# The convolution's bias as a row of its bands, its windows in parts of 32 and 30 rows, and LayerNorm's affine part on VectorE

## The chip, the cores and the metric

The kernel is one program on one core of a Trainium2 chip. The metric is the device time of one execution in microseconds (us), as the median of several runs; smaller is better.

## What is computed

The reference is one inference step of a two-layer backbone: 256 context tokens and 1024 latent tokens, model width 1024. The change lies in the first (even) layer, in its convolution branch and in what stands around it:

```python
a_u, a_g, a_z, b_q, b_k, b_v, b_z = jnp.split(h @ w_in, SPLIT_E, axis=-1)   # A_W = 512 each, b_*: 512 each
a = a_u * jax.nn.sigmoid(a_g)
a = lax.conv_general_dilated(a, conv_w[:, None, :], window_strides=(1,),     # CONV_K = 31, one filter a channel
                             padding=[(15, 15)], dimension_numbers=('NWC', 'WIO', 'NWC'),
                             feature_group_count=A_W) + conv_b
a = jax.nn.silu(layer_norm(a, ln_g, ln_b)) * jax.nn.silu(a_z)
...
o = over_query_blocks(lambda qb: diff_attend(qb, keys, vals, lam), q)        # from b_q, b_k, b_v
return jnp.concatenate([a, o * jax.nn.silu(b_z)], axis=-1) @ w_out

def layer_norm(x, g, b):
    mu, var = mean(x), mean(square(x - mu))
    return (x - mu) * rsqrt(var + 1e-6) * g + b
```

The second layer and all attention code are the same in both kernels.

## The kernel before

The tokens are ten tiles of 128 (tiles 0 and 1 context, 2 to 9 latent). The input stage of the first layer is `l0_in`. It multiplies the normed tokens with seven groups of weight columns: two groups `ug0` and `ug1` (a_u and a_g of 256 channels each), `az` (weights `w6`), and four heads (weights `w2` to `w5`). Each group is eight 128x512 weight chunks; each chunk is loaded by SP (`raw_w`, L263), rounded by ScalarE (L269), and its low part is cut by GpSimd (`w_w`, L270). TensorE works unit by unit: a unit is one token tile (or one channel block) and has 24 matmuls into one of five `acc` buffers of PSUM, three for each chunk (L318 to L320, or L330 to L332). The names in a profile row are `acc_v` (a head's value and gate columns of a token tile), `acc_p` (a context tile), `acc_c` (channel blocks of q and k). A unit's result is taken out of PSUM by ScalarE (`cn` L492, `vz` L509) and VectorE (`gz` L340, `ch` L494 and L495), which frees the buffer. `hl` (L357) is VectorE's part of the split of a context tile's q and k, which TensorE transposes (`tr_st`, L360).

Between the units a generator is stepped (`filler`, `branch`): first `conv`, at 4/3 step a unit, then `ln_steps`, at `LNR` steps a unit. `modulation` vectors for later stages (`md_v`, `modv`, L162, from `rawm_v` loads) are stepped beside it.

`conv` works in eight blocks `q` of 64 channels. The gated values, split in a high and a low part, are stored to DRAM (`AW0`, `AW1`; `ahl` L416 and L417, store L420, two `ahl` buffers) with padding rows. `windows(q)` loads windows of 64 rows, 32 rows apart, 21 times 2 of them, back into SBUF (`X`, two buffers): high parts in partitions 0 to 63, low parts in 64 to 127, in four DMAs. A band matrix (`band`, built on the host from the filter) has 64 rows of which 62 are not zero, and 32 columns; one matmul for each channel (L471) gives 32 outputs of each window. ScalarE and VectorE add the two halves (`cy`, L476 and L477), and ScalarE's queue stores the block to DRAM (`CV`). The values stay doubled there, since the gate is computed as (tanh + 1) times u.

`ln_steps` then loads CV by token tile (`lnw`, L571), and for each tile: halves it and adds the bias `convb` (L575), statistics (L577, L579, L580) and the root on GpSimd (`mv`, L95), `norm` (VectorE L586, ScalarE L587, GpSimd L588), tanh on ScalarE (L609), two gate multiplications on VectorE (L592, L593; the second reads `AZ`, loaded at L585), store to `CAT` (L594).

The program is written out once and a scheduler orders the instructions of each engine with its own simulated times; a queue keeps its order. SP's DMAs use eight completion semaphores in turn, so a DMA also waits for the one eight places ahead.

Of the kernel before, what the change touches and what calls it, by code (L numbers as in the profile page):

```python
# [10 lines left out]
F32 = mybir.dt.float32  # L11
F32R = mybir.dt.float32r
# [20 lines left out]
def f32(ap):  # L33
    return ap.bitcast(F32)
# [42 lines left out]
class K:  # L77
# [323 lines left out]
    def l0_in(self, ws, raw, wp, cxp, p1, small, acc, pst, mod, freed):  # L401
# [8 lines left out]
        def ug_units(gi):  # L410
# [10 lines left out]

            return [(f"ug{gi}_{t}", self.mm_tok(t), lambda ps, t=t: done(t, ps)) for t in TORD]

        def conv():

            raws, bands = [], []  # L430

            def windows(q):
                x = cxp.tile([128, CWIN, CCH], F32R, tag="X", bufs=2, name=f"X{q}")
                cs = slice(q % 4 * CCH, q % 4 * CCH + CCH)
                for o in range(2):
                    for hl in range(2):
                        src = self.AW[q // 4][hl, 32 * o : 32 * o + 32 * CWIN, cs].rearrange("(j r) c -> r j c", r=64)
                        dst = x[hl * 64 : hl * 64 + 64].rearrange("p (j o) c -> p o j c", o=2)[:, o]
                        nc.sync.dma_start(f32(dst), f32(src))
                return x  # L440

            def load_taps():
                if len(raws) < 32:
                    raws.append(self.wload(a["toep"][len(raws)], raw, f"band{len(raws)}", "rawb"))

            def cut_taps():
                i = len(bands)
                if i < 32:
                    bands.append(self.wcut(raws[i], cxp, f"band{i}", "band", nc.vector))
                    load_taps()  # L450

            load_taps()
            load_taps()
            yield
            xs = [windows(0)]
            cut_taps()
            yield
            yield
            for q in range(8):
                y = cxp.tile([CWIN, 32, CCH], F32, tag="cy", bufs=1, name=f"cy{q}")  # L460
                x = xs.pop(0)
                for c0 in range(0, CCH, 8):
                    if c0 == 8 and q < 7:
                        xs.append(windows(q + 1))
                    ps = pst(f"cv{q}_{c0}")
                    for i in range(8):
                        c = c0 + i
                        if c % 16 == 0:
                            cut_taps()
                        w = bands[4 * q + c // 16]  # L470
                        nc.tensor.matmul(  # L471
                            ps[0:CWIN, i * 64 : i * 64 + 64].rearrange("p (a m) -> p a m", a=2), x[:, :, c],
                            w[:, :, c % 16 * 32 : c % 16 * 32 + 32], start=True, stop=True)
                    pv = ps[0:CWIN].rearrange("p (c a m) -> p c a m", a=2, m=32)
                    yv = y[:, :, c0 : c0 + 8].rearrange("p m c -> p c m")
                    nc.scalar.copy(yv, pv[:, :, 1])  # L476
                    nc.vector.tensor_tensor(yv, pv[:, :, 0], yv, ALU.add)  # L477
                    if c0 + 8 == CCH:
                        dst = self.CV[:, q * CCH : q * CCH + CCH].rearrange("(w m) c -> w m c", m=32)
                        nc.scalar.dma_start(dst, y)  # L480
                    yield
# [75 lines left out]
        def ln_steps():  # L557

            con = cxp.tile([128, 3, 512], F32, tag="cy", bufs=1, name="lncon")
            for i, nm in enumerate(("lng", "lnb", "convb")):
                nc.sync.dma_start(con[:, i], a[nm].broadcast_to([128, 512]))
            ws = [cxp.tile([128, CWIN * CCH], F32, tag="X", bufs=2, name=f"lnw{i}") for i in range(2)]
            slots = [w[:, i * 512 : i * 512 + 512] for w in ws for i in range(5)]
# [6 lines left out]

            def stats(t):
                u = us[t % 6]
                nc.vector.scalar_tensor_tensor(u, u, 0.5, con[:, 2], ALU.mult, ALU.add)  # L575
                st = small.tile([128, 6], F32, tag="bn", name=f"bn{t}")
                nc.vector.bn_stats(st, u)  # L577
                mvs[t] = mv = small.tile([128, 4], F32, tag="mv", bufs=3, name=f"mv{t}")
                nc.vector.bn_aggr(mv[:, 0:2], st)  # L579
                nc.vector.tensor_scalar(mv[:, 1:2], mv[:, 1:2], EPS, None, ALU.add)  # L580
                self.rsq(mv[:, 2:3], mv[:, 1:2])

            def norm(t):
                u, mv = us[t % 6], mvs[t]
                nc.sync.dma_start(azs[t % 2], self.AZ[t])  # L585
                nc.vector.scalar_tensor_tensor(u, u, mv[:, 0:1], con[:, 0], ALU.subtract, ALU.mult)  # L586
                nc.scalar.activation(u, u, AF.Identity, scale=mv[:, 2:3])  # L587
                nc.gpsimd.tensor_tensor(u, u, con[:, 1], ALU.add)  # L588

            def gate(t):  # L590
                u = us[t % 6]
# [4 lines left out]
            load(0)  # L596
            yield
            load(1)
            yield
            yield  # L600
            for s in range(NT + 3):
                if s >= 3:
# [8 lines left out]
                    stats(s)  # L611
                yield

        convd, credit, RATE, LNR = [], [0.0], 4 / 3, 0.8

        def branch():
            yield from conv()
# [864 lines left out]
def _layout(i):  # L1482
# [38 lines left out]
    band = np.zeros((512, 64, 32), np.float32)  # L1521
    for m in range(32):
        band[:, m : m + 31, m] = i["a_conv_w"][0].T
    band = band.reshape(32, 16, 64, 32).transpose(0, 2, 1, 3).reshape(32, 64, 512)
    z["toep"] = c(np.concatenate([band, band], 1))
    z["convb"] = c(i["a_conv_b"])
    z["lng"], z["lnb"] = c(i["a_ln_g"]), c(i["a_ln_b"])
    z["lamv"] = c(i["b_lambda"][0])
    z["subg"] = c(i["b_subln_g"])
# [52 lines left out]
```

## Time and profile before

| | before |
|---|---|
| time, median of 3 runs | 1827.05 us (1825.0 to 1831.14) |
| time of the profiled execution | 1820.6 us |
| span in its profile | 1818.8 us |
| mean granted TensorE clock | 0.987 |
| busy: TensorE, VectorE, ScalarE, GpSimd | 95%, 68%, 53%, 43% |
| first matmul of the convolution | 137.86 us |
| LayerNorm's first and last instruction on VectorE | 427.22 and 486.37 us |

The times in a profile count from the span's start. A row of the timeline gives start, duration, engine, line, operation, output and input, and in brackets how long the engine had idled before and what released it; in a row of several instructions (x2, x6) the duration covers all. A row of a window gives the busy time of each engine in that stretch, the granted clock (1.00 is full speed), the DMA engines' busy share and GB/s. A group of instructions gives the count, the busy sum in us, the mean of one in ns, and the idle time before them.

### The profile page before, as it was taken

Reading aid. Unit: us, or ns where it says so; the run is one execution under the profiler, and the core shown is the slowest. Engines: PE = TensorE matmul, PEld = TensorE weight load, DVE = VectorE, ACT = ScalarE, POOL = GpSimd, SP = SyncE. Lnnn points to the kernel's source line nnn. Section 1 sums busy time; section 2 is a strip of 40 time slices with the busy share of each in tenths; the row PEclk is TensorE's granted clock in tenths of the full one; section 3 lists DMA queues with packets and bytes.
Section 4 is the critical chain, followed back from the end, with each engine's and each line's share of the span. In section 5 each row is a group of like instructions: output and inputs, shape, how many; then the busy total and the mean of one; then the engine's idle time right before and its main releaser. Section 6 shows DMA issues by size and latency. Waiting matters only on the chain. (4 is left out here: it accounts for less than half of the span.)

```text
span 1818.8 us, 28268 instructions
## 1 busy us (share of the span) xinstructions
PE 1727.2 (95%) x9434; PEld 1420.3 (78%) x9434; DVE 1235.8 (68%) x2935; ACT 972.9 (53%) x2060; POOL 787.8 (43%) x706
## 2 busy tenths in 40 slices
PE   5999999998899999989999999999999999999998
PEld 2787888887777778778887778877888888878786
DVE  7656765676749989925476672118899989999322
ACT  6433344342437778743344533227777888898311
POOL 3321032233627778754138873203344334354332
PEclk9999999999899999999999999999999999999999
DMA  8468888854774433144246345253122114141441
GB/s 304 156 159 198 240 199 186 190 171 140 220 202 112 124 102 96 45 161 152 85 157 183 138 133 157 76 147 100 33 54 58 33 41 108 59 146 58 153 174 52
DMA packets 220277, 241.23 MB, mean 133 GB/s; under 512 B 72128, under 2 KB 154848, under 8 KB 219876
## 3 DMA queue, kind: packets, MB, share of 16 engines
q1 hardware_dynamic: 207476, 233.53, 44.1%
q0 software_dynamic: 1792, 3.15, 0.8%
q10 hardware_dynamic: 10864, 2.75, 0.8%
q8 instruction: 75, 1.23, 0.3%
q14 instruction: 70, 0.57, 0.1%
HBM read 169.08 MB, written 70.28 MB: 132 GB/s over the span
## 5 line engine op out<-in xcount | busy, mean ns | idle before, releaser
L397 ACT ACTIVATE E<-E,mm 128x1536 f32<-128x1536 f32 (+3 forms) x240 | 293.6, 1227 | 59.8 <-DVE E L394 49.9
L270 POOL TENSOR_TENSOR w_w<-raw_w,w_w 128x512 fp32r<-128x512 f32 x88 | 127.1, 1453 | 237.4 <-ACT w_w L269 180.1
L1238 PE MATMUL S<-k1d,q1s 128*128 128x512 f32 (+1 forms) x704 | 206.9, 390 | 4.0 <-DMA q1s<-qT 1.7
L372 POOL TENSOR_TENSOR el<-ef,eh 128x512 fp32r<-128x512 f32 x96 | 124.2, 1295 | 187.7 <-DVE eh L371 182.7
L394 DVE TENSOR_SCALAR_CACHE_REDUCE E<-S,mm 128x512 f32<-128x512 f32 x256 | 190.2, 744 | 12.9 <-PE S L798 3.9
L1168 PE MATMUL wt_et<-ident,E 128*128 128x128 f32 x1264 | 186.1, 273 | 3.7 <-ACT E L397 3.2
L1168 PEld LDWEIGHTS wt_et<-ident,E 128*128 128x128 f32 x1264 | 153.8, 140 | 37.2 <-ACT E L397 4.5
L368 DVE TENSOR_TENSOR el<-wt_et,eh 128x512 fp32r<-128x512 f32 x220 | 146.9, 682 | 10.2 <-ACT eh L367 9.6
L1238 PEld LDWEIGHTS S<-k1d,q1s 128*128 128x128 f32 x704 | 121.4, 190 | 28.5 <-DVE E L394 7.7
L367 ACT CAST eh<-wt_et 128x512 fp32r<-128x512 f32 x220 | 124.3, 595 | 29.1 <-PE wt_et L1168 28.6
L1163 PE MATMUL pv_pv<-el,v 128*128 128x512 f32 x316 | 138.9, 440 | 0.5 <-POOL el L372 0.4
L798 PE MATMUL S<-kd,qs 128*128 128x512 f32 (+1 forms) x416 | 131.6, 422 | 7.8 <-DVE E L394 3.7
L318 PE MATMUL acc_g<-w_w,hi 128*128 128x512 f32 x336 | 131.4, 393 | 1.4 <-DVE v L1021 1.3
L319 PE MATMUL acc_g<-w_w,hi 128*128 128x512 f32 x336 | 132.2, 394 | 0.5 <-POOL w_w L270 0.5
L320 PE MATMUL acc_g<-w_w,lo 128*128 128x512 f32 x336 | 131.7, 392 | 0.0
L1162 PE MATMUL pv_pv<-eh,v 128*128 128x512 f32 x316 | 127.8, 405 | 0.5 <-DVE eh L371 0.5
L873 PE MATMUL acc_po<-wo,oh 128*128 128x512 f32 x320 | 126.2, 395 | 0.0
L874 PE MATMUL acc_po<-wo,oh 128*128 128x512 f32 x320 | 125.5, 393 | 0.0
L394 DVE TENSOR_SCALAR_CACHE_REDUCE E<-S 128x512 f32<-128x512 f32 (+1 forms) x160 | 99.8, 630 | 18.9 <-PE S L1238 12.3
L269 ACT CAST w_w<-raw_w 128x512 fp32r<-128x512 f32 x96 | 59.0, 620 | 90.7 <-DMA raw_w<-in_we 22.7
L877 PE MATMUL acc_po<-wo,ol 128*128 128x512 f32 x320 | 103.1, 393 | 0.0
L798 PEld LDWEIGHTS S<-kd,qs 128*128 128x128 f32 x416 | 67.6, 191 | 30.8 <-DVE E L394 20.9
(294 smaller groups left out, 4550.4 us busy)
## 6 DMA issues: line engine op xcount, KB each, us to landing
rawm_v<-in_wmodt SPq DMA_DIRECT2D x64, 256.0 KB, 2.9
raw_w<-in_we SPq DMA_DIRECT2D x56, 256.0 KB, 3.5
X<-AW SPq DMA_DIRECT2D x32, 336.0 KB, 6.4
qs<-QK SPq DMA_DIRECT2D x80, 128.0 KB, 2.8
ac<-CAT SPq DMA_DIRECT2D x20, 512.0 KB, 4.0
raw_w<-in_wod SPq DMA_DIRECT2D x40, 256.0 KB, 2.7
q1s<-qT SPq DMA_DIRECT2D x40, 256.0 KB, 2.6
xraw_m<-in_wmod SPq DMA_DIRECT2D x32, 256.0 KB, 4.6
```

Source lines behind the costliest of these rows:

```text
L270: (eng or nc.gpsimd).tensor_tensor(w[:, 1, :], r, f32(w[:, 0, :]), ALU.subtract)
L318: nc.tensor.matmul(ps[:, o:], a, w[:, 0, o:], start=(k == 0), stop=False)
L319: nc.tensor.matmul(ps[:, o:], a, w[:, 1, o:], start=False, stop=False)
L320: nc.tensor.matmul(ps[:, o:], b, w[:, 0, o:], start=False, stop=(k == KC - 1))
L368: nc.vector.tensor_tensor(lo, ps, f32(hi), ALU.subtract)
L394: nc.vector.tensor_scalar(e[:, o : o + w], S, -1.0, init, ALU.mult, ALU.min, accum_out=m[:, i : i + 1])
L397: nc.scalar.activation(e[:, :n], e[:, :n], AF.Exp, bias=init, scale=-1.0, accum_out=s)
L798: nc.tensor.matmul(S, q[:, hl], kd[:, c, kofs + o : kofs + o + n], start=(hl == 0), stop=(hl == 1))
L1162: nc.tensor.matmul(pv, vs, wh, start=(i == 0), stop=False)
L1163: nc.tensor.matmul(pv, vs, wl, start=False, stop=(i == nk - 1))
L1168: nc.tensor.transpose(ps[:, g * 128 : g * 128 + 128], E[g][:, ec : ec + 128], self.ident)
L1238: nc.tensor.matmul(S, qs[:, g, :], kd[hl][:, kc : kc + n], start=(hl == 0), stop=(hl == 1))
```

## The change

The bias moves into the band matrix: row 62 of each channel's band, in the high half and the low half alike, holds the channel's bias, and the windows hold 2.0 in row 62 of the high half and 0.0 in row 62 of the low half. The convolution's output is then twice (convolution + bias) without another instruction. The window buffers are allocated once and their rows 32 to 63 and 96 to 127 filled by GpSimd; the window loads leave rows 62 and 63 untouched, and each of the four loads is cut into rows 0 to 31 and 32 to 61. LayerNorm works on the doubled values with four times the epsilon, so that halving and adding the bias go away (and with them the load of `convb`); scale and bias of `norm` become one VectorE instruction in the place of one on ScalarE and one on GpSimd. `LNR` goes from 0.8 to 0.6, and one empty step is left out.

```diff
+        win = [cxp.tile([128, CWIN, CCH], F32R, tag="X", bufs=2, name=f"win{i}") for i in range(2)]
+        for w in win:
+            nc.gpsimd.memset(f32(w[32:64]), 2.0)
+            nc.gpsimd.memset(f32(w[96:128]), 0.0)
...
             def windows(q):
-                x = cxp.tile([128, CWIN, CCH], F32R, tag="X", bufs=2, name=f"X{q}")
+                x = win[q % 2]
...
-                        nc.sync.dma_start(f32(dst), f32(src))
+                        for r in (slice(0, 32), slice(32, 62)):
+                            nc.sync.dma_start(f32(dst[r]), f32(src[r]))
...
-            con = cxp.tile([128, 3, 512], F32, tag="cy", bufs=1, name="lncon")
-            for i, nm in enumerate(("lng", "lnb", "convb")):
+            con = cxp.tile([128, 2, 512], F32, tag="cy", bufs=1, name="lncon")
+            for i, nm in enumerate(("lng", "lnb")):
...
             def stats(t):
                 u = us[t % 6]
-                nc.vector.scalar_tensor_tensor(u, u, 0.5, con[:, 2], ALU.mult, ALU.add)
...
-                nc.vector.tensor_scalar(mv[:, 1:2], mv[:, 1:2], EPS, None, ALU.add)
+                nc.vector.tensor_scalar(mv[:, 1:2], mv[:, 1:2], 4 * EPS, None, ALU.add)
...
                 nc.vector.scalar_tensor_tensor(u, u, mv[:, 0:1], con[:, 0], ALU.subtract, ALU.mult)
-                nc.scalar.activation(u, u, AF.Identity, scale=mv[:, 2:3])
-                nc.gpsimd.tensor_tensor(u, u, con[:, 1], ALU.add)
+                nc.vector.scalar_tensor_tensor(u, u, mv[:, 2:3], con[:, 1], ALU.mult, ALU.add)
...
             load(1)
             yield
-            yield
             yield
...
-        convd, credit, RATE, LNR = [], [0.0], 4 / 3, 0.8
+        convd, credit, RATE, LNR = [], [0.0], 4 / 3, 0.6
...
     band = np.zeros((512, 64, 32), np.float32)
     for m in range(32):
         band[:, m : m + 31, m] = i["a_conv_w"][0].T
+    band[:, 62] = i["a_conv_b"][0][:, None]
...
-    z["convb"] = c(i["a_conv_b"])
```

The scheduler gives another order in `l0_in` alone. On GpSimd the four fills (128 partitions in two parts of 32, 2688 values each) come between the cuts of weight chunks 4 and 5 of group `ug1`; on TensorE the matmuls of chunks 5 to 7 for the token tiles 2 to 4 of that group stand some 40 matmuls further back, and the first convolution block 6 matmuls further ahead (row 440, before 446).

Three more places. First SP's queue at the first window loads. Before (`X0`, `X1` are the windows, `ahl1_2` and `ahl1_3` stores that free the buffers of `ahl1_4` and `ahl1_5`):

```order
L420 DMA AW0_73<-ahl0_0_1092 128x2x256
L263 DMA raw_w6_2_1494<-in_we 128x512
L420 DMA AW0_73<-ahl0_1_1099 128x2x256
L261 DMA rawm_v0_2_4_0_1362<-in_wmodt 128x512
L261 DMA rawm_v0_2_5_0_1416<-in_wmodt 128x512
L439 DMA X0_1135<-AW0_73 64x21x64 x4
L439 DMA X1_1281<-AW0_73 64x21x64 x2
L420 DMA AW1_74<-ahl1_2_1131 128x2x256
L439 DMA X1_1281<-AW0_73 64x21x64
L420 DMA AW1_74<-ahl1_3_1184 128x2x256
L439 DMA X1_1281<-AW0_73 64x21x64
L261 DMA rawm_v0_2_6_0_1481<-in_wmodt 128x512
```

Now, from the last two of 16 window loads on:

```order
L446 DMA win1_740<-AW0_73 32x21x64
L446 DMA win1_740<-AW0_73 30x21x64
L261 DMA rawm_v0_2_5_0_1428<-in_wmodt 128x512
L261 DMA rawm_v0_2_6_0_1493<-in_wmodt 128x512
L263 DMA raw_w6_0_1502<-in_we 128x512
L263 DMA raw_w6_1_1504<-in_we 128x512
L263 DMA raw_w6_2_1506<-in_we 128x512
L420 DMA AW1_74<-ahl1_2_1137 128x2x256
L420 DMA AW1_74<-ahl1_3_1193 128x2x256
```

Two `rawm_v` loads, the three first loads of group `w6` and the two `AW1` stores now stand behind all the window loads.

Second, VectorE from LayerNorm's first instruction on. The row to look for is `gz2_6` (L340), which frees the buffer of `acc_v2_6`. Before, the last 12 rows up to it (27 LayerNorm and `ch` rows stand ahead of it in all):

```order
L577 BN_STATS bn3_4582<-lnw0_4291 128x6
L575 SCALAR_TENSOR_TENSOR lnw1_4292<-lnw1_4292,lncon_4287 128x512
L592 SCALAR_TENSOR_TENSOR lnw0_4291<-lnw1_4292,lnw0_4291 128x512
L579 BN_AGGR mv2_4534<-bn2_4532 128x2
L494 TENSOR_TENSOR ch2_2_1_4431<-cn2_2_1_4473,ropeT_526 128x512
L495 TENSOR_TENSOR ch2_2_0_4430<-cn2_2_1_4473,ropeT_526 128x512
L579 BN_AGGR mv3_4584<-bn3_4582 128x2
L593 SCALAR_TENSOR_TENSOR lnw0_4291<-lnw0_4291,lnw1_4292 128x512
L580 TENSOR_SCALAR mv2_4534<-mv2_4534 128x1
L586 SCALAR_TENSOR_TENSOR lnw0_4291<-lnw0_4291,mv2_4534,lncon_4287 128x512
L577 BN_STATS bn4_4645<-lnw0_4291 128x6
L340 SCALAR_TENSOR_TENSOR gz2_6_4519<-th_z2_6_4520,acc_v2_6_4491 128x128
```

Now (L592 is the first half of `norm`, the new L593 the second; L597 and L598 are the gate):

```order
L583 BN_STATS bn4_4699<-lnw0_4320 128x6
L583 BN_STATS bn5_4829<-lnw1_4321 128x6
L597 SCALAR_TENSOR_TENSOR lnw0_4320<-lnw1_4321,lnw0_4320 128x512
L598 SCALAR_TENSOR_TENSOR lnw0_4320<-lnw0_4320,lnw1_4321 128x512
L501 TENSOR_TENSOR ch2_2_1_4459<-cn2_2_1_4499,ropeT_526 128x512
L502 TENSOR_TENSOR ch2_2_0_4458<-cn2_2_1_4499,ropeT_526 128x512
L593 SCALAR_TENSOR_TENSOR lnw0_4320<-lnw0_4320,mv2_4558,lncon_4317 128x512
L593 SCALAR_TENSOR_TENSOR lnw0_4320<-lnw0_4320,mv3_4606,lncon_4317 128x512
L585 BN_AGGR mv4_4701<-bn4_4699 128x2
L340 SCALAR_TENSOR_TENSOR gz2_6_4545<-th_z2_6_4546,acc_v2_6_4517 128x128
```

`gz2_6` has 30 rows ahead of it instead of 27: 6 statistics (L583), 5 aggregates (L585), 4 one-column additions (L586), 4 first and 4 second halves of `norm`, 3 gate rows and 4 `ch` rows. The `hl` row of the second context tile of head 3 comes 57 rows after `gz2_6`, before 58.

Third, GpSimd where the chunks `w_w5` of the last head are cut among LayerNorm's roots (`mv`). Before:

```order
L95 TENSOR_TENSOR mv4_4647<-mv4_4647,mhalf_65 128x1
L270 TENSOR_TENSOR w_w5_0_4598<-raw_w5_0_4592,w_w5_0_4598 128x512
L270 TENSOR_TENSOR w_w5_1_4615<-raw_w5_1_4594,w_w5_1_4615 128x512
L95 TENSOR_TENSOR mv5_4697<-mv5_4697,mhalf_65 128x1
L270 TENSOR_TENSOR w_w5_2_4632<-raw_w5_2_4596,w_w5_2_4632 128x512
L588 TENSOR_TENSOR lnw0_4291<-lnw0_4291,lncon_4287 128x512
L588 TENSOR_TENSOR lnw1_4292<-lnw1_4292,lncon_4287 128x512
L270 TENSOR_TENSOR w_w5_3_4665<-raw_w5_3_4613,w_w5_3_4665 128x512
L95 TENSOR_TENSOR mv6_4745<-mv6_4745,mhalf_65 128x1
L270 TENSOR_TENSOR w_w5_4_4682<-raw_w5_4_4630,w_w5_4_4682 128x512
L270 TENSOR_TENSOR w_w5_5_4715<-raw_w5_5_4663,w_w5_5_4715 128x512
```

Now:

```order
L95 TENSOR_TENSOR mv4_4701<-mv4_4701,mhalf_65 128x1
L95 TENSOR_TENSOR mv5_4831<-mv5_4831,mhalf_65 128x1
L270 TENSOR_TENSOR w_w5_0_4620<-raw_w5_0_4614,w_w5_0_4620 128x512
L270 TENSOR_TENSOR w_w5_1_4637<-raw_w5_1_4616,w_w5_1_4637 128x512
L270 TENSOR_TENSOR w_w5_2_4654<-raw_w5_2_4618,w_w5_2_4654 128x512
L95 TENSOR_TENSOR mv6_4896<-mv6_4896,mhalf_65 128x1
L270 TENSOR_TENSOR w_w5_3_4671<-raw_w5_3_4635,w_w5_3_4671 128x512
L270 TENSOR_TENSOR w_w5_4_4688<-raw_w5_4_4652,w_w5_4_4688 128x512
L270 TENSOR_TENSOR w_w5_5_4719<-raw_w5_5_4669,w_w5_5_4719 128x512
```

The additions L588 are gone from between the cuts, and the first cut comes one root later.

## The prediction

> **What bounds the kernel now.** I read the page's busy shares first, then TensorE's waits in the stretch of LayerNorm, then that stretch by windows, then the queues row by row.
>
> ```profile
> span 1818.8 us, 28268 instructions
> PE 1727.2 (95%) x9434; PEld 1420.3 (78%) x9434; DVE 1235.8 (68%) x2935; ACT 972.9 (53%) x2060; POOL 787.8 (43%) x706
> ```
>
> TensorE sets the time, so an edit on another engine counts only where TensorE waits for it. The change adds no matmul and takes none away; only TensorE's waits and its clock can move the time. The waits from 430 to 490 us (engine, line, releaser: us, times, longest):
>
> ```profile
> PE acc_v L318 <- DVE gz L340: 6.2, 1, 6.2
> PE acc_c L332 <- POOL w_w L270: 3.7, 2, 2.4
> PE tr_st L360 <- DVE hl L357: 2.5, 1, 2.5
> PE acc_v L318 <- ACT cn L492: 0.7, 1, 0.7
> ```
>
> That is 13.1 us. The clock falls after them, and VectorE is full meanwhile:
>
> ```profile
> 460.00:480.00 20.00, 15.65 (x63) 11.69 (x61) 19.59 (x31) 10.52 (x34) 15.78 (x13) 0.83 0.73 254
> ...
> 444.00:448.00 4.00, 3.65 (x15) 3.45 (x16) 4.00 (x9) 2.02 (x3) 2.89 (x3) 0.50 0.83 260
> ...
> 464.00:468.00 4.00, 2.35 (x6) 1.05 (x5) 3.96 (x7) 2.41 (x12) 4.00 (x4) 0.68 0.92 344
> 468.00:472.00 4.00, 3.94 (x9) 3.15 (x10) 4.00 (x10) 2.23 (x8) 2.64 (x3) 0.50 0.70 228
> ```
>
> (Busy us of TensorE, weight loads, VectorE, ScalarE, GpSimd, then the clock.) At clock 0.50, 3.65 us of matmuls lose 1.8; with 2.35 times 0.32 = 0.75 and 3.94 times 0.5 = 2.0 that makes 4.5 us. So 13.1 + 4.5 = 17.6 us is what LayerNorm's stretch can give back in all.
>
> **The change, part by part.**
>
> *LayerNorm on VectorE.* Rows of VectorE's timeline:
>
> ```profile
> 427.22 0.69 DVE L575 SCALAR_TENSOR_TENSOR lnw<-lnw,lncon 128x512 f32<-128x512 f32 x1 [9.80 <-DMA lnw<-CV]
> 427.94 0.69 DVE L577 BATCH_NORM_STATS2 bn<-lnw 128x6 f32<-128x512 f32 x1
> 428.55 0.67 DVE L575 SCALAR_TENSOR_TENSOR lnw<-lnw,lncon 128x512 f32<-128x512 f32 x1
> 429.15 0.17 DVE L579 BATCH_NORM_AGGREGATE mv<-bn 128x2 f32<-128x6 f32 x1
> 429.26 0.69 DVE L577 BATCH_NORM_STATS2 bn<-lnw 128x6 f32<-128x512 f32 x1
> 429.87 0.14 DVE L580 TENSOR_SCALAR mv<-mv 128x1 f32<-128x1 f32 x1
> 429.93 0.74 DVE L586 SCALAR_TENSOR_TENSOR lnw<-lnw,mv,lncon 128x512 f32<-128x512 f32 x1
> ...
> 432.48 1.69 DVE L575 SCALAR_TENSOR_TENSOR lnw<-lnw,lncon 128x512 f32<-128x512 f32 x1
> ...
> 444.04 0.26 DVE L340 SCALAR_TENSOR_TENSOR gz<-th_z,acc_v 128x128 f32<-128x128 f32 x1
> ...
> 459.79 1.08 DVE L593 SCALAR_TENSOR_TENSOR lnw<-lnw,lnw 128x512 f32<-128x512 f32 x1 [3.64 <-DMA lnw<-AZ]
> ...
> 481.70 0.41 DVE L357 TENSOR_TENSOR hl<-nat,hl 128x256 fp32r<-128x256 f32 x1
> ```
>
> Each tile loses one such instruction (L575, 0.60 us from start to start) and gains one (the new L593, priced as L586, 0.66): nothing in work. Three things do move.
>
> First, the start. VectorE waits until 427.22 for loads.
>
> ```profile
> 419.80 0.36 SPq L571 DMA_DIRECT2D lnw<-CV  x1
> ...
> lnw<-CV SPq DMA_DIRECT2D x6, 256.0 KB, 5.0
> ```
>
> The tile lands at about 419.8 + 5.0 = 424.8, 2.4 us before the row starts; I lay the rest on the third constants load (`convb`), which L575 needs and nothing needs now. The new first instruction reads the tile alone. With half a us less of issue ahead, LayerNorm starts at about 424.5: 2.7 us earlier. Bounds: 0 (the tile itself was late) and 2.9.
>
> Second, the long instructions. A 128x512 instruction takes 0.69 us, or some 1.7 when GpSimd works beside it, as at 432.48, 0.6 us into this addition:
>
> ```profile
> 431.92 1.71 POOL L588 TENSOR_TENSOR lnw<-lnw,lncon 128x512 f32<-128x512 f32 x1 [0.84 <-ACT lnw L587]
> ...
> L588 POOL TENSOR_TENSOR lnw<-lnw,lncon 128x512 f32<-128x512 f32 x10 | 15.6, 1566 | 3.3 <-ACT lnw L587 3.3
> L270 POOL TENSOR_TENSOR w_w<-raw_w,w_w 128x512 fp32r<-128x512 f32 x8 | 14.1, 1769 | 0.0
> ...
> L575 DVE SCALAR_TENSOR_TENSOR lnw<-lnw,lncon 128x512 f32<-128x512 f32 x10 | 10.0, 996 | 9.8 <-DMA lnw<-CV 9.8
> ...
> L593 DVE SCALAR_TENSOR_TENSOR lnw<-lnw,lnw 128x512 f32<-128x512 f32 x9 | 9.2, 1023 | 3.9 <-DMA lnw<-AZ 3.9
> L592 DVE SCALAR_TENSOR_TENSOR lnw<-lnw,lnw 128x512 f32<-128x512 f32 x9 | 8.1, 896 | 0.1
> ```
>
> (The groups are of 427 to 488 us.) Against 0.69 these three groups are long by 10 x 0.31 + 9 x 0.33 + 9 x 0.21 = 8.0 us, and they are 28 of some 43 instructions of this size with two tile inputs there, so by count some 12 us in all. The additions L588 are 15.6 of the 29.7 us in the two GpSimd groups, so their share would be 6; I take 5. Bounds: 0 (the cuts of `w_w5` just hit as many rows) and 8.
>
> [...]
>
> Third, order: `hl` stands 2 rows later (1.2 us lost). The 3.64 us wait for `AZ` goes if its load, which waits for the gate two tiles before to free its buffer, moves ahead with the rest; whether it does the rows don't tell, so I take half: 1.8, bounds 0 and 3.6.
>
> VectorE thus reaches `hl` 2.7 + 5 - 1.2 + 1.8 = 8.3 us earlier.
>
> *TensorE in the same stretch.* It can use this only if its own waits shrink too. `gz2_6`: 30 rows ahead are 6 x 0.61 + 5 x 0.11 + 4 x 0.06 + 8 x 0.66 + 7 x 0.60 = 13.9 us, plus about 2 for the two `ch` additions left on GpSimd: 424.5 + 15.9 = 440.4 instead of 444.04, 3.6 earlier. Six matmuls that followed this wait now go ahead of it, 1.0 us. So 6.2 becomes 1.6. The `w_w5` waits:
>
> ```profile
> 452.30 5.00 POOL L270 TENSOR_TENSOR w_w<-raw_w,w_w 128x512 fp32r<-128x512 f32 x2
> ...
> 464.60 3.04 POOL L270 TENSOR_TENSOR w_w<-raw_w,w_w 128x512 fp32r<-128x512 f32 x2
> ```
>
> Chunks 4 and 5 end at 467.6, with three additions (4.6 us) ahead of them since 452.30. Without these, and with VectorE ahead by 4 to 5 us, they end at about 458, before TensorE asks: 3.7 us gone (bounds 0 and 3.7). Of the 4.5 us at a low clock I take 3 as gone, as the two longest waits go. TensorE's side adds up to 4.6 + 3.7 + 3 = 11.3 us. The smaller side decides: VectorE's 8.3. TensorE then simply waits some 3 us longer at `hl`, which becomes the last wait of the stretch.
>
> *The fills.* GpSimd is between two cuts of `ug1`:
>
> ```profile
> 108.86 1.29 POOL L270 TENSOR_TENSOR w_w<-raw_w,w_w 128x512 fp32r<-128x512 f32 x1 [0.16 <-ACT w_w L269]
> ...
> L405 POOL MEMSET z<- 64x512 f32 x1 | 0.5, 515 | 0.0
> ...
> masks.py:197 POOL MEMSET ident<- 128x128 f32 x1 | 0.2, 205 | 0.3 <-POOLq L1561 0.3
> ...
> 123.07 0.39 PE L318 MATMUL acc_ug<-w_w,hi 128*128 128x512 f32 x1
> 123.30 0.40 PE L319 MATMUL acc_ug<-w_w,hi 128*128 128x512 f32 x1
> ...
> 137.86 1.36 PE L471 MATMUL tr_cv<-band_band,X 128*42 128x64 f32 x16 [0.40 <-DMA X<-AW]
> ```
>
> 384 more values took 0.31 us: 0.81 ns each, so 2688 take 0.515 + 1.76 = 2.3 us and four fills 9.1: 110.15 to 119.3, chunk 5 cut by 120.6. TensorE first needs it at row 405, 41 rows ahead of row 446, where the convolution began at 137.86 less its 0.40: 137.5 - 41 x 0.233 = 127.9. Cover 7.3 us: cost nothing. At the price of the addition-like row at 108.86 (1.29 us for 512) four fills take 27.1 and chunk 5 comes at 138.5, a wait of 10.6: the upper bound. I take the fill's own row.
>
> *The first windows.* The convolution now starts 6 matmuls earlier, 1.4 us, while its window lands when it did: a wait of 0.4 + 1.4. Cost 1.4, bounds 0 and 5 (next part). Later windows are loaded a block ahead: nothing.
>
> *`LNR` and the empty step* cost nothing by themselves: LayerNorm's last rows stand where they stood among VectorE's rows.
>
> **Sum.** -8.3 + 1.4 = -6.9 us against the profiled execution's 1820.6, that is 1813.7; against the median of the runs, 1827.05, it gives 1820. A difference under 0.3%, 5.5 us, can't be told from none.
>
> **Rivals.**
>
> *The stretch gives all.* If the additions return more of VectorE than 5 us, and the `AZ` wait goes, TensorE's side binds and the clock stays up: 13.1 + 4.5 less about 3.5 that stay, plus 1.4: -12.7, 1814. [...] Here two waits of under 2.4 us each were enough for 0.50 at 468. Chance 0.16.
>
> *Nothing comes of it.* The start is set by the tile's landing, and the cuts, now back to back, lengthen as many rows. Then only `w_w5`'s wait turns into one for VectorE: -1, 1826. For it: the same VectorE work, and 19.59 busy of 20. Against: 15.6 us of GpSimd's work do go. Chance 0.27.
>
> *The fills are slow*: -8.3 + 1.4 + 10.6, about +4: 1831. Against it stands a fill's own row. Chance 0.04.
>
> *The doubled window loads hold SP* (slower):
>
> ```profile
> 126.80 9.18 SPq L439 DMA_DIRECT2D X<-AW  x6
> ...
> 141.28 2.56 SPq L261 DMA_DIRECT2D rawm_v<-in_wmodt  x2
> ...
> 148.16 1.30 DVE L477 TENSOR_TENSOR cy<-tr_cv,cy 42x256 f32<-42x256 f32 x2
> ```
>
> Six whole loads took 9.18 us to issue, 1.53 each. If a half costs as much, 16 take 24.5, to 151.3 instead of 141.3. Behind them stand the `rawm_v` loads, for which VectorE waits ahead of the `cy` rows of 148.16; these come at about 156, while TensorE needs their PSUM buffers at about 152. So 4 to 5 us there, and up to 6.1 us of SP at each of the seven further window loads, with the stores that free `ahl`, `ch` and `vz` buffers behind. At 3 us for each of the eight loads it would be 24 against 8.3: +16, 1843. It decides from (8.3 + 5.5) / 8 = 1.7 us a load. Against it: if issue goes by bytes, a half costs half. Chance 0.13.
>
> **Chances and range.** The forecast's own case, 1816 to 1824, has 0.40; 0.25 of that lies under 1821.5. Faster: 0.25, 0.16 of "all" and 0.04 of "nothing", whose lower end reaches there: 0.45. Same: 0.15, 0.23 of "nothing" and 0.02 of the slow fills: 0.40. Slower: the other 0.02 of these and 0.13: 0.15. The range leaves out the best half of "all" and most of the slow case: 1811 to 1831.
>
> **What would show it.** Right: LayerNorm's first row near 424.5 (less the shift of what is ahead), rows of 0.69 us where 1.7 stood, `gz2_6` some 16 us later, no wait for `w_w`, a longer one for `hl`, clock above 0.9 from 440 to 470. Wrong: fills of over 4 us each; a `tr_cv` wait over 3 us near 150; window loads at 1.5 us each on SP; a new wait in the stretch for `AZ` or `CV` loads.

## The result and the profile after

| | before | after |
|---|---|---|
| time, median | 1826.58 us (4 runs, 1825.0 to 1831.14) | 1812.7 us (4 runs, 1811.37 to 1818.01) |
| profiled execution, span | 1820.6, 1818.8 us | 1813.53, 1811.5 us |
| mean granted TensorE clock | 0.987 | 0.989 |
| first matmul of the convolution | 137.86 us | 135.19 us |
| LayerNorm's first instruction on VectorE | 427.22 us | 424.62 us |

The ratio after to before is 0.9929, 95% interval [0.9914, 0.9944]: faster by 13.9 us. The forecast was 1820.0 with a range of 1811 to 1831. The changed kernel run again (e1, below) gave 0.9948 [0.9928, 0.9968], 10.8 us.

The page of the changed kernel, first lines:

```profile
span 1811.5 us, 28282 instructions
PE 1726.2 (95%) x9434; PEld 1419.1 (78%) x9434; DVE 1227.6 (68%) x2935; ACT 965.7 (53%) x2050; POOL 780.4 (43%) x700
```

TensorE's busy time is 1.0 us less (1726.2 against 1727.2), the rest of its span 6.3 us less (85.3 against 91.6): over these two profiles the gain lies mostly in waits. TensorE's waits from 428 to 490 us of the changed kernel:

```profile
PE acc_v L318 <- DVE gz L340: 3.6, 1, 3.6
PE tr_st L360 <- DVE hl L357: 2.4, 1, 2.4
PE acc_c L330 <- ACT nat L534: 0.8, 1, 0.8
PE acc_c L332 <- POOL w_w L270: 0.4, 1, 0.4
```

These are 7.2 us where 13.5 stood (the 13.1 of the prediction and a wait of 0.4 for `nat` that its list leaves out): 6.3 back. One window over the stretch, 424 to 490 us, shows the clock (columns as in the prediction); first of before, then of after:

```profile
424.00:490.00 66.00, 52.54 (x282) 44.83 (x281) 58.19 (x95) 26.91 (x65) 43.90 (x31) 0.87 0.58 189
```

```profile
424.00:490.00 66.00, 58.79 (x333) 51.44 (x332) 55.52 (x104) 22.27 (x62) 30.57 (x24) 0.92 0.70 206
```

The clock is 0.92 instead of 0.87, and GpSimd is busy 13 us less in this window. The window of after holds more matmuls (333 against 282), so for the sum I take the same matmuls in both traces, those from 2325 to 2600 (431 to 497 us before). TensorE is idle for 13.5 us between them before and 7.2 after, and busy for 52.1 and 49.9: 6.3 us of waits and 2.2 of clock.

VectorE's timeline of after, at the places of the prediction:

```profile
424.62 1.30 DVE L583 BATCH_NORM_STATS2 bn<-lnw 128x6 f32<-128x512 f32 x2 [8.24 <-DMA lnw<-CV]
...
436.97 3.43 DVE L593 SCALAR_TENSOR_TENSOR lnw<-lnw,mv,lncon 128x512 f32<-128x512 f32 x2
...
440.42 0.25 DVE L340 SCALAR_TENSOR_TENSOR gz<-th_z,acc_v 128x128 f32<-128x128 f32 x1
...
473.22 0.42 DVE L357 TENSOR_TENSOR hl<-nat,hl 128x256 fp32r<-128x256 f32 x1
```

`gz2_6` came at 440.42 where 440.4 was forecast, but not quite for the reasons given: the two traces are already 2.3 us apart by matmul 300, ahead of any edit. I therefore compare executions by TensorE's count of matmuls, which is 9434 in both kernels: the time from one matmul to another in both traces, the places of this table being the same numbers in each. TensorE's order differs between the two kernels from matmul 436 to 2733 and is the same elsewhere. Differences to the profile of before, in us:

| stretch (matmuls; about when) | after | again (e1) | before again (e10) |
|---|---|---|---|
| 0 to 450 (to 120 us) | -2.3 | -1.0 | -3.0 |
| 450 to 600, start of the convolution | +2.1 | -0.3 | +0.2 |
| 600 to 2080, blocks of the convolution | +2.0 | +1.5 | +3.4 |
| 2080 to 2175 (390 to 409 us) | -2.7 | -4.0 | +0.8 |
| 2175 to 2325 | -0.1 | -0.1 | 0 |
| 2325 to 2600, LayerNorm (431 to 497 us) | -8.5 | -10.2 | -1.4 |
| 2600 to 2750, the last place where the order differs (to 525 us) | +1.5 | +6.2 | +2.9 |
| 2750 to the end, same order | +1.0 | +3.0 | -2.0 |

So there are two places of gain: LayerNorm's stretch, as forecast, and 2.7 to 4.0 us near 400 us, of which the prediction said nothing. The last two rows show how far such numbers carry. From 2600 to 2750 there is one more wait for an `hl` (matmul 2691 after, 2689 before: 2.3 us in after, 4.6 in e1, 0.5 in before, 2.3 in e10), so a part of what LayerNorm's stretch gave may be lost again there; with 2.9 us in the unedited kernel these profiles don't say how much. From 2750 on the order is the same, and still the executions differ by up to 5 us. The profiled execution of before (1820.6 us) was faster than all four timed ones, so the spans differ by only 7.3 us where the medians differ by 13.9.

The second place. SP and VectorE, and then TensorE, in the kernel before:

```profile
395.19 0.42 SPq L261 DMA_DIRECT2D rawm_v<-in_wmodt  x1
...
399.79 0.70 DVE L162 CUSTOM_DVE_ANT_0 md_v<-rawm_v,cr(0, 2)_1_2586 128x512 f32<-128x512 f32 x1 [5.83 <-DMA rawm_v<-in_wmodt]
...
401.89 0.42 DVE L357 TENSOR_TENSOR hl<-nat,hl 128x256 fp32r<-128x256 f32 x1
...
402.36 0.66 PE L360 MATMUL tr_st<-ident,hl 128*128 128x128 f32 x4 [2.84 <-DVE hl L357]
...
404.00:408.00 4.00, 4.00 (x26) 4.00 (x24) 2.40 (x4) 1.11 (x3) 0.57 (x1) 0.57 0.76 214
```

SP issues the last `rawm_v` load behind stores of `vz`, `gz` and `kv`; VectorE waits 5.83 us for it, with the `hl` of the second context tile of head 1 queued behind its two modulation rows and a `ch` row; TensorE waits 2.84 us for `hl`, and runs at 0.57 afterwards (1.7 us lost of 4.00). The same in the changed kernel, where the first two `hl` and `tr_st` rows are of the first context tile and the last two of the second:

```profile
391.04 0.33 SPq L261 DMA_DIRECT2D rawm_v<-in_wmodt  x1
...
395.34 0.69 DVE L162 CUSTOM_DVE_ANT_0 md_v<-rawm_v,cr(0, 2)_1_2607 128x512 f32<-128x512 f32 x1
...
397.58 0.42 DVE L357 TENSOR_TENSOR hl<-nat,hl 128x256 fp32r<-128x256 f32 x1
...
398.05 0.66 PE L360 MATMUL tr_st<-ident,hl 128*128 128x128 f32 x4 [0.84 <-DVE hl L357]
...
400.32 0.43 DVE L357 TENSOR_TENSOR hl<-nat,hl 128x256 fp32r<-128x256 f32 x1
...
403.14 0.60 PE L360 MATMUL tr_st<-ident,hl 128*128 128x128 f32 x4
...
404.00:408.00 4.00, 4.00 (x43) 4.00 (x42) 1.54 (x3) 1.97 (x5) 0.63 (x1) 1.00 0.60 186
```

The load goes out ahead of those stores, 4.2 us earlier, or 5.9 us counted against TensorE's matmul 2080, which comes 1.8 us later in this trace. VectorE's wait of 5.83 us is gone, the second tile's `hl` is there before TensorE asks, and the clock stays full. But the modulation rows now stand ahead of the first tile's `hl`, for which TensorE waits 0.84 us at matmul 2099; before, it did not wait there. Counted from matmul 2100 the place would thus be worth 5.0 us in after and in e1, which is the number that the expectations below speak of; from 2080, with that wait in, it is 2.7 and 4.0. No instruction of this place was edited. The scheduler's order on SP and VectorE moved.

### The profile page after: what moved, and what is told of

Its sections match the earlier page's. It is cut to its first block, busy times and chain, and to the rows that moved or that the text cites. A ratio compares the mean times of both kernels' runs of the same rounds, so it can differ in the third digit from the quotient of the medians.

```text
span 1811.5 us, 28282 instructions
## 1 busy us (share of the span) xinstructions
PE 1726.2 (95%) x9434; PEld 1419.1 (78%) x9434; DVE 1227.6 (68%) x2935; ACT 965.7 (53%) x2050; POOL 780.4 (43%) x700
## 4 chain that ended last, share of the span: by engine, by line
PE 36%; DVE 6%; POOL 3%; DMA 2%; issue 2%; ACT 1%; SPq 0%; POOLq 0%; DVEq 0%; ACTq 0%
PE S L1242 6%; PE wt_et L1172 6%; PE pv_pv L1167 3%; PE pv_pv L1166 3%; PE acc_g L318 3%; PE acc_g L319 3%; PE acc_g L320 3%; PE acc_po L881 2%; PE acc_po L877 2%; PE acc_po L878 2%; DVE E L394 1%; DVE el L368 1%; POOL mtv L165 1%; PE wt_oo L1191 1%; POOL hss_q L95 1%
## 5 line engine op out<-in xcount | busy, mean ns | idle before, releaser
L394 DVE TENSOR_SCALAR_CACHE_REDUCE E<-S 128x512 f32<-128x512 f32 (+1 forms) x160 | 99.9, 630 | 17.7 <-PE S L1242 10.9
```

Of the source, the lines that this page charges most:

```text
L394: nc.vector.tensor_scalar(e[:, o : o + w], S, -1.0, init, ALU.mult, ALU.min, accum_out=m[:, i : i + 1])
```

## The experiments

The theory after these two profiles: the gain has two parts, less GpSimd work beside VectorE in LayerNorm's stretch (from the affine edit, chiefly) and the load order on SP near 400 us (from the bias edit). The rivals: the earlier start of LayerNorm, or the hand-over from VectorE to ScalarE to GpSimd that the affine edit takes away, or the new `LNR`, or chance in the clock. There were twelve runs, two of them of the two kernels unedited. "LN" below is the stretch from matmul 2325 to 2600 against the first profile of before (after: -8.5), "400" that from 2080 to 2175 (after: -2.7).

**e1**, the changed kernel unedited.

> The changed kernel once more, without any edit. Theory A (the gain is LayerNorm's stretch alone, some 7 to 9 us, and the rest of the 13.9 us between the medians is spread between executions): a median 7 to 12 us under that of before in these runs, and a profile in which LayerNorm's stretch ends 8 to 10 us earlier than it began to differ, with stretches outside it differing by up to 3 us either way. Theory B (the whole 14 us belong to the change): 13 to 15 us under before, and a profile with a second place of 5 us or more that is always better.

1815.44 us, 0.9948 [0.9928, 0.9968]; LN -10.2, 400 -4.0. The 10.8 us between the medians are what theory A expected, the second place what theory B did. Both places come back; the clock's luck does not explain them.

**e2**, the affine part alone, on the kernel before:

```diff
-                nc.scalar.activation(u, u, AF.Identity, scale=mv[:, 2:3])
-                nc.gpsimd.tensor_tensor(u, u, con[:, 1], ALU.add)
+                nc.vector.scalar_tensor_tensor(u, u, mv[:, 2:3], con[:, 1], ALU.mult, ALU.add)
```

> Before, with only LayerNorm's scale and bias made one VectorE instruction (L593's form); bias load, halving instruction L575, whole window loads and 0.8 step a unit stay. VectorE gets ten instructions more (6.6 us). Theory A (GpSimd's ten additions lengthen VectorE's rows by about 5 us): the two nearly cancel, +1 us at hl, but the w_w waits (3.7 us) go: -4 to +2 us against before. Rival (what counts is the missing hand-over from VectorE to ScalarE to GpSimd): -6 us or better. Second rival (VectorE's instruction count binds): +5 us or worse.

1818.2 us, 0.9964 [0.9947, 0.9981]; LN -8.8, 400 +1.2. LayerNorm's first row on VectorE in this kernel, and two of TensorE's waits from 418 to 495 us:

```profile
429.26 0.69 DVE L575 SCALAR_TENSOR_TENSOR lnw<-lnw,lncon 128x512 f32<-128x512 f32 x1 [9.75 <-DMA lnw<-CV]
...
PE acc_v L318 <- DVE gz L340: 3.9, 1, 3.9
PE acc_c L332 <- POOL w_w L270: 0.6, 1, 0.6
```

LayerNorm starts where it did relative to TensorE (1.2 us ahead of matmul 2300; before 1.2, after 2.7). So the earlier start belongs to the bias edit, and the stretch's gain does not need it. TensorE still waits 3.2 us for `hl` near 400. The median is 8.0 us under that of before, and the ratio gives 6.6 (interval 3.5 to 9.7): more than theory A expected (4 at most, which the interval still reaches), and what the first rival did, the missing hand-over. VectorE's ten instructions more did not cost what they take, although its long instructions got shorter by only 2.9 us in sum (counted as under *The long instructions* below). How the stretch's gain divides between the hand-over and the shorter instructions is not shown; e9 tests the instructions alone.

**e3**, the bias, the windows and the epsilon alone (the changed kernel with ScalarE's scale and GpSimd's addition put back, `LNR` 0.8 and the empty step).

> The changed kernel with LayerNorm's scale on ScalarE and its bias addition on GpSimd again, at 0.8 step a unit and with the empty step: the bias in the bands, the fills and the split window loads alone. VectorE loses ten instructions (6 us) against before and starts LayerNorm 2 to 3 us earlier. Theory A: hl some 8 us earlier, less what the additions still lengthen, +2.4 at the first windows: -4 to -7 us against before. Rival (the additions on GpSimd set the stretch): no more than -2 us, with the w_w waits of 3 us or more still there.

1816.51 us, 0.9960 [0.9944, 0.9976]; LN -7.0, 400 -2.5, with waits of 0.8 us each for the first tile's `hl` and for a `gz`, as in after (0.8 and 0.5), and none for the second tile's. The place at 400 comes with this part of the change and not with the affine part. In LayerNorm's stretch each part alone gives most of what both give (-7.0 and -8.8 against -8.5 and -10.2): they do not add up. The affine part's gain is the sturdier: counted on to matmul 2750 it is 8.2 us of 8.8, that of this part 1.4 of 7.0. But the profiled execution of e3 took 1823.1 us, 6.6 more than its median, so its stretches are a poor sample.

**e4**, the changed kernel with one number back:

```diff
-        convd, credit, RATE, LNR = [], [0.0], 4 / 3, 0.6
+        convd, credit, RATE, LNR = [], [0.0], 4 / 3, 0.8
```

> The changed kernel with 0.8 instead of 0.6 step a unit. Theory A (the rate only feeds the scheduler, and the order hardly depends on it): within 2 us of the changed kernel. Rival (the lower rate is what spreads LayerNorm and frees TensorE): 4 us or more slower than the changed kernel, with gz and hl waits of over 6 us together.

1816.43 us, 0.9953 [0.9934, 0.9971], beside e1's 0.9948 on the same chip; LN -10.6, 400 -4.0.

**e6**, the kernel before with `LNR` 0.6.

> Before with LayerNorm at 0.6 instead of 0.8 step a unit, nothing else. Theory A (the rate hardly changes the order): within 3 us of before, gz wait of 5 us or more at 444. Rival (the rate is part of the gain): -5 us or more.

1825.28 us, 0.9998 [0.9982, 1.0015]; LN +0.1, 400 +2.3; TensorE's `gz` wait is 6.3 us, as before. `LNR` does nothing that these runs could show in either kernel. TensorE's order in e6 is that of before, matmul for matmul, and between e4 and after at least 98% of each engine's rows up to 560 us stand in the same order: the scheduler puts the rows in nearly the same order whatever step they were written at.

**e5**, the kernel before with the modulation of the first head stepped twice as fast, so that its loads come ahead of the stores without the change:

```diff
-            (2, lambda: head_units(0), hd, filler(RATE, 1)),
+            (2, lambda: head_units(0), hd, filler(RATE, 2)),
```

> Before, with two instead of one step of the modulation vectors a unit in head 0, so that their last loads (rawm_v) and the VectorE rows that wait for them lie ahead of about 380 us. It tests the second place that the traces show: before, VectorE waits 5.8 us for the last rawm_v load with the hl row of head 1 behind it, and TensorE waits 2.8 us at 402 and then runs at a low clock; with the bias in the bands that load stands ahead of the stores in SP's queue. Theory A (this wait alone is worth the 5 us by which rows 394 to 409 differ): no hl wait over 1 us near 400, TensorE 4 to 5 us ahead there, LayerNorm's stretch as before, -3 to -6 us in time. Rival (the place is a swing between executions, or the wait moves to another row): within 2 us of before.

1823.0 us, 0.9989 [0.9974, 1.0003]; 400 -4.8 with no TensorE wait there at all, LN -0.2. The place at 400 can be cleared by moving these loads, and the VectorE rows that wait for them, alone. In the time it does not stand out: other stretches of its profile took the gain back (+7.5 us after matmul 2600), and the interval reaches from 4.7 us faster to 0.5 slower.

**e11** is e2 with e5's edit: affine part and earlier modulation, but no bias in the bands and whole window loads.

> Before with LayerNorm's scale and bias in one VectorE instruction and two steps of the modulation vectors a unit in head 0: neither bias in the bands nor split windows. Theory A (the gain is the two places, however they are cleared): -5 us near 400 and -8 to -9 us in LayerNorm's stretch, -8 to -13 us against before, as the changed kernel. Rival (LayerNorm's stretch in it lasts longer, since VectorE has ten instructions more and starts later): no better than the affine edit alone, -7 us or less.

1813.72 us, 0.9945 [0.9926, 0.9963]; LN -9.4, 400 -4.8. Its waits from 385 to 495 us:

```profile
PE acc_v L318 <- DVE gz L340: 3.3, 1, 3.3
PE acc_c L332 <- POOL w_w L270: 2.1, 2, 1.2
...
PE tr_st L360 <- DVE hl L357: 0.5, 1, 0.5
```

This is the changed kernel's time without the bias edit. So what the bias edit gave beyond the affine part can be had from the place of a few loads, as far as the stretches show it; the times of e11 and e2 can't be told apart, since their intervals overlap.

**e12** is the changed kernel with e5's edit, to see whether its place at 400 has more to give.

> The changed kernel with two steps of the modulation vectors a unit in head 0, the best of the two edits together. Theory A (both places are already cleared in the changed kernel, so that the step has nothing left to clear): within 2 us of the changed kernel, LayerNorm's stretch 55 to 57 us of TensorE, hl wait under 1 us near 400. Rival (VectorE's waits for rawm_v loads still hold the convolution's cy rows): 3 us or more faster than the changed kernel, with tr_cv waits under 4 us.

1812.39 us, 0.9931 [0.9906, 0.9955]: the same as the changed kernel. 400 -4.8, with no wait left there; LN -6.3 with a wait of 4.1 us for `hl`.

**e7**, the changed kernel with two modulation steps a unit in the group `az` (`filler(RATE, 2)` there).

> The changed kernel with two steps of the modulation vectors a unit in the az group, so that their rows end well ahead of head 1. If VectorE's waits for rawm_v loads still cost TensorE something in the changed kernel (cy rows of the convolution behind them, 6.9 us of tr_cv waits), it is 2 to 5 us faster than the changed kernel; if the rows moved crowd the convolution's own rows, as many us slower.

1815.81 us, 0.9937 [0.9916, 0.9959]: no different from the changed kernel; 400 -4.8, LN -10.3. Neither e12 nor e7 beats it.

**e9**, the changed kernel with ten additions on GpSimd which nobody reads, in the place of the ones taken away:

```diff
-            con = cxp.tile([128, 2, 512], F32, tag="cy", bufs=1, name="lncon")
+            con = cxp.tile([128, 3, 512], F32, tag="cy", bufs=1, name="lncon")
...
                 nc.vector.scalar_tensor_tensor(u, u, mv[:, 2:3], con[:, 1], ALU.mult, ALU.add)
+                nc.gpsimd.tensor_tensor(con[:, 2], con[:, 0], con[:, 1], ALU.add)
```

> The changed kernel with ten 128x512 additions on GpSimd that nobody reads or waits for (constants' sum into a third constants row), which the scheduler puts between LayerNorm's first roots. Theory A (an addition on GpSimd lengthens VectorE's two-input rows beside it): 13 to 16 us of additions around 424 to 440, at least six VectorE rows of 1.6 us or more there instead of two, gz2_6 3 to 8 us later, TensorE's gz wait 6 us or more, 2 to 6 us slower than the changed kernel. Rival (what the changed kernel saved there was only the hand-over through ScalarE and GpSimd): gz2_6 no more than 1 us later, since these additions have no successor.

1830.58 us, 1.0025 [1.0010, 1.0040]: by the ratios 14 to 18 us slower than the changed kernel, where 2 to 6 were expected. In LayerNorm's stretch it loses 11.4 against after (+2.9 against before). Its rows show how:

```profile
428.11 4.66 POOL L594 TENSOR_TENSOR lncon<-lncon 128x512 f32<-128x512 f32 x3
...
428.26 1.69 DVE L501 TENSOR_TENSOR ch<-cn,ropeT 128x512 f32<-128x512 f32 x1
...
431.66 1.66 DVE L593 SCALAR_TENSOR_TENSOR lnw<-lnw,mv,lncon 128x512 f32<-128x512 f32 x1
...
445.28 0.28 DVE L340 SCALAR_TENSOR_TENSOR gz<-th_z,acc_v 128x128 f32<-128x128 f32 x1
```

Nothing waits for these additions by data. They need only constants, so they run early and in bunches, and VectorE's rows of 128x512 with two tile inputs took 1.62 to 1.78 us beside them from 428 to 441 us. From LayerNorm's first row to `gz2_6` it is 22.6 us (after 15.8). TensorE's waits from 422 to 495 us follow:

```profile
PE acc_v L318 <- DVE gz L340: 5.2, 1, 5.2
PE tr_st L360 <- DVE hl L357: 4.6, 1, 4.6
PE acc_v L318 <- ACT cn L499: 3.3, 1, 3.3
PE acc_c L332 <- POOL w_w L270: 2.2, 1, 2.2
```

Against the rival that the additions cost nothing by themselves, this settles that they cost VectorE its time, and TensorE through it: the excess of its long instructions, counted as under *The long instructions* below, is 15.8 us, against 7.7 in after. `w_w` waits more too; the cuts stand behind LayerNorm's roots, which wait for VectorE. The 11.4 us are more than the 8.5 by which the whole change shortened this stretch. The rest of the loss, 9.1 us of it after matmul 2600, lies where no addition runs and I do not ascribe it to them.

**e8**, the changed kernel with each window load whole, 62 rows in one DMA:

```diff
-                        for r in (slice(0, 32), slice(32, 62)):
+                        for r in (slice(0, 62),):
```

> The changed kernel with each window load as one DMA of rows 0 to 61 instead of two of 32 and 30 rows. [...] Rival (the cut costs or gains nothing but SP's issue time): within 3 us of the changed kernel, SP some 4 us shorter at the first windows.

2041.39 us, 1.1176 [1.1152, 1.1199]. The same loads on SP, in the changed kernel and in this one:

```profile
124.46 13.98 SPq L446 DMA_DIRECT2D win<-AW  x16
```

```profile
125.09 48.32 SPq L446 DMA_DIRECT2D win<-AW  x6
...
PE tr_cv L478 <- DVE cy L484: 130.4, 15, 30.9
PE tr_cv L478 <- DMA win<-AW: 31.4, 1, 31.4
```

In the mean of the first loads, one of 62 rows holds SP for 8.05 us, one of 32 or 30 rows for 0.87, and one of 64 rows (before) for 1.53. The very first takes 0.26, 0.32 and 0.68 us; those of 62 rows behind it take 9.2 to 9.9 us each. The cost is not one of bytes: 62 rows are 325.5 KB, 64 are 336.0. The loads of 62 rows landed 12 to 24 us after their issue began; the parts of 32 and 30 rows took 3.5 to 6.4. From 146 to 166 us, with such loads alone in SP's queue, the DMA engines move 35 GB/s at a busy share of 0.16, against 168 GB/s at 1.30 from 126 to 138 us in the changed kernel. What in a count of 62 rows makes them slow is not shown. So the cut into two parts is no tuning of its own; without it row 62 for the bias costs 12%.

**e10**, the kernel before unedited, one run with a profile.

> Before once more for a second profile. Theory A (stretches without an edit swing by some us between executions, the two places near 400 and from 430 to 490 do not): the same waits of 2 to 3 us for hl near 400 and of about 6 us for gz, and a TensorE that is 3 to 8 us later than in the first profile of before by the end of the span, lost outside these places. Rival: the same within 1 us at every place, and the first profile is the ordinary one.

1821.95 us; LN -1.4, 400 +0.8. Its waits from 385 to 495 us are those of before:

```profile
PE acc_v L318 <- DVE gz L340: 6.2, 1, 6.2
PE tr_st L360 <- DVE hl L357: 5.2, 2, 4.0
PE acc_c L332 <- POOL w_w L270: 3.9, 2, 2.5
```

So both places are the kernel's, not the first profile's, and LayerNorm's stretch repeats within 1.4 us. At the span's end TensorE is only 1.3 us later than in the first profile, not the 3 to 8 that theory A expected. Nor does a late TensorE hide the wait near 400: in e1 and e4 matmul 2080 comes only 0.2 us later than in the first profile of before, and the place is 4.0 us shorter all the same.

The stretches can be held against the times. The sum from matmul 2080 to 2750 holds both places and the wait behind them; all numbers are in us, the sums against the first profile of before, the medians against the runs of before beside them:

| | after | e1 | e4 | e7 | e12 | e11 | e2 | e3 | e5 | e6 | e9 |
|---|---|---|---|---|---|---|---|---|---|---|---|
| 2080 to 2750 | -9.8 | -8.1 | -11.2 | -14.2 | -12.2 | -14.0 | -7.1 | -4.0 | -2.1 | +2.5 | +4.1 |
| median | -13.9 | -10.8 | -9.8 | -10.9 | -15.7 | -11.9 | -8.0 | -9.7 | -3.7 | -1.5 | +5.0 |

In e10 the sum is +2.3. The two rows agree within 6 us, so these places make up most of the change in time, and a few us stay unassigned in each.

## Why the prediction was right, and where it was not

The sign, the range and the size of LayerNorm's stretch held. The gain, 13.9 and 10.8 us, was twice and one and a half times the 6.9 of the sum, and that 1812.7 lies inside the range is owed to the rival "the stretch gives all" (1814), for which the range was drawn so low. Its mechanism is not what happened: the stretch gave about what the forecast's own case said (-8.5 and -10.2 for -8.3), and the rest came from elsewhere. So the number fell into the range partly by luck.

*The step that failed* is the view of the waits: it was read from 430 to 490 us only, and the order of SP's modulation loads, of which the prediction says nothing, was thereby costed at nothing. It was worth 2.7 and 4.0 us in the two profiles of the changed kernel, and 4.8 in e5. The wait stood in the trace of before (2.84 us for `hl`, 5.83 us of VectorE for `rawm_v`), and the order of the changed kernel had the `rawm_v` load ahead of the stores. Reading every TensorE wait of over 2 us in `l0_in`, and the order around each, would have found it. e3 and e5 against e2 and e6 show the cause: the place of these loads and of the rows that wait for them, moved by the bias edit.

*LayerNorm's start*: 2.7 us forecast, 1.6 measured (first row against matmul 2300: from 1.2 us ahead to 2.7 ahead in after, 2.9 in e1; 1.7 in e10). The reading behind it was wrong: it laid the late start on the load of `convb`, but the bracket of that row, [9.80 <-DMA lnw<-CV], names the tile's own load, and in the trace `convb` had landed 0.7 us ahead of it (426.4 against 427.1). What moved is the tile: its load is issued 0.6 us earlier against matmul 2300, with one constants load fewer ahead of it, and the row starts 6.4 us after that issue instead of 7.4. e2, with `convb`, starts late, but e5, with `convb` too, starts 2.0 us ahead, so that load alone does not set the start; why the tile lands sooner is not shown.

*The long instructions*: 5 us forecast, 2.9 measured. From LayerNorm's first row to the second `hl`, VectorE's 128x512 instructions with two tile inputs were 10.6 us longer than 0.74 us each before (11 of them over 1.3 us), and 7.7 after (7 of them). The groups of after, 424 to 482 us, show what is left:

```profile
L593 DVE SCALAR_TENSOR_TENSOR lnw<-lnw,mv,lncon 128x512 f32<-128x512 f32 x10 | 12.3, 1244 | 0.4 <-POOL mv L95 0.4
L592 DVE SCALAR_TENSOR_TENSOR lnw<-lnw,mv,lncon 128x512 f32<-128x512 f32 x10 | 7.4, 740 | 0.0
L270 POOL TENSOR_TENSOR w_w<-raw_w,w_w 128x512 fp32r<-128x512 f32 x8 | 12.4, 1571 | 0.4 <-ACT w_w L269 0.4
L583 DVE BATCH_NORM_STATS2 bn<-lnw 128x6 f32<-128x512 f32 x10 | 6.7, 685 | 8.2 <-DMA lnw<-CV 8.2
```

The cuts of `w_w` and the `ch` additions now stand beside the new L593 (1244 ns). The count of rows gave 6 as the additions' share; the lower bound named the reason for less, that the cuts hit other rows, and half of it came true.

*The `AZ` wait*: 1.8 forecast. VectorE's idle time between its rows there went from 4.2 to 1.5 us: 2.7. *Order*: -1.2 as counted. These terms make `hl` 1.6 + 2.9 + 2.7 - 1.2 = 6.0 us earlier; measured from matmul 2325 it is 7.45, and I cannot assign the remaining 1.4.

*TensorE's side*: up to 11.3 forecast, 6.3 of waits and 2.2 of clock measured, 8.5. `gz` fell to 3.6 instead of 1.6: the start came 1.1 us less early, and a wait of 0.7 for `cn` ahead of it went, so that TensorE came sooner. From LayerNorm's first row `gz2_6` took 15.8 us, as its rows had been added up (15.9). `w_w` fell to 0.4 where 0 was forecast, and `hl` stayed at 2.4 where it was to grow by some 3. So neither side clearly bound the other: both came out near 8.

*The fills*: right. On GpSimd of the changed kernel:

```profile
107.88 2.34 POOL L426 MEMSET win<- 32x2688 f32 x1
...
115.06 2.34 POOL L427 MEMSET win<- 32x2688 f32 x1
117.49 4.43 POOL L270 TENSOR_TENSOR w_w<-raw_w,w_w 128x512 fp32r<-128x512 f32 x3
```

2.3 us each was forecast, and no wait for chunk 5 follows.

*The first windows*: 1.4 forecast, not borne out as a cost. TensorE's row:

```profile
135.19 0.76 PE L478 MATMUL tr_cv<-band_band,win 128*42 128x64 f32 x8 [1.46 <-issue]
...
136.00:140.00 4.00, 4.00 (x18) 3.19 (x18) 2.24 (x4) 1.83 (x4) 0.00 (x0) 0.58 1.32 162
```

A wait of 1.46 is there; its bracket names no load, but in the trace the last of the first window's eight loads landed at 135.0. A low clock follows it (0.58) that the term left out: +2.1 from matmul 450 to 600 in this profile. But the other runs with the same windows have -0.5 to +1.0 there, and e11, without the edit, has +2.5, so no cost of it is shown. *SP held by twice the loads*: refuted, 0.87 us for a half against 1.53 for a whole, so SP is held for 13.98 us for sixteen where 24.5 was feared.

*`LNR`*: nothing, as forecast (e4, e6).

What stays open: the convolution's blocks (600 to 2080) differ by -1.3 to +5.8 us between kernels (e8 left aside), and by +3.4 in the unedited one, and the code from matmul 2750 on, where TensorE's order is the same in all but e5, e11 and e12, by -2.0 to +6.3; I found no cause for either that these runs could separate. Open too is how much of LayerNorm's gain is lost again at the `hl` behind it, and how the affine part's gain divides between shorter instructions and the missing hand-over. The swings limit what a single profile can say, and for that reason verdicts above go by medians and by stretches.

## What to carry to other kernels

Read TensorE's waits over the whole part of the program that a scheduler will order anew, not only where the edited instructions stand: an order can change a load's place in a queue 30 us ahead of the edit, and that was about a quarter of the gain in the two places. Work on GpSimd that nobody waits for was not free here: beside a VectorE that was busy for all 20 us from 424 to 444 us in e9, ten such additions made LayerNorm's stretch 11.4 us longer than in after. Count whose instructions such work lengthens, and whether other GpSimd work will take its place. To compare two profiles whose matmuls are the same in number, go by matmul count, stretch by stretch, take a second profile of the unchanged kernel to see which stretches swing by themselves, and do not let a stretch begin or end beside a wait: putting such a bound 20 matmuls earlier made 2.7 us of 5.0 here.

## What the runs showed that was not expected

DMAs of 62 rows held SP's queue for 8.05 us in the mean of the first loads (e8), where 64 rows took 1.53 (before) and 32 or 30 rows 0.87 (after). Ten additions that nothing depends on cost 11 us of TensorE's time in one stretch of 66 us, more than the whole change gained there; the scheduler put them early and in bunches. VectorE's statistics instruction, with one input of the same size, was not longer in e9 beside the additions: 683 ns in the mean, and 685 in after. And each of two edits alone gave most of the gain of their stretch up to matmul 2600, so that neither's share can be stated.
